# ple_gate's sixth product, right columns: its sums of weights made in DRAM during the output projection, not grown from the second product's

## The chip, the cores and the metric

The kernel runs on one core of one Trainium2 chip. The metric is the device time of one execution in microseconds; lower is better.

## The reference

One layer of a trunk: 512 tokens, width 2048, all in float32. Cut to the two matrix products that matter here, sliding-window attention ends in an output projection, and a gate with a second weight matrix of the same size follows.

```python
x = x + (out * silu(gate)) @ w_out            # [512,2048] @ [2048,2048]: the output projection
emb = p @ ple_proj                            # [512,256] @ [256,2048]
g = sigmoid(rmsnorm(x, ple_norm) @ ple_gate)  # [512,2048] @ [2048,2048]: the ple_gate product
x = x + emb * g
return rmsnorm(x, final_g)
```

## The kernel before

**Stages.** The kernel projects q, k, v and the gates and runs the attention between these products (to about 450 us), then does the output projection with `w_out` (450 to 621 us), then the product with `ple_gate` (621 to about 771 us), and stores the rows. In the second half PE works without a break through one list of pieces.

**Seven products instead of eight.** Each of the two big products is cut into 2x2 blocks and made by seven block products (Strassen's scheme in Winograd's form). Each block product needs a sum or difference of blocks of the activations and of the weights. The products are numbered 1 to 7; product 2 is left to a second level of the same scheme (`Small`, pieces half as long). The others run in the order `ORDER_OUT = ORDER_PLE = (1, 7, 6, 5, 3, 4)`; for each there is a left column half (`jj` = 0) and a right one (`jj` = 1), and for each half four pieces of weights (`m` = 0 to 3) of 128x1024 elements, 512 KB. So "7,1,2" is product 7, right columns, third piece. A full piece feeds 12 matmuls of 128x512, a small one 6.

**How a piece comes to PE.** The weights are float32 and the matmuls take a rounded high part and a remainder. A piece is loaded by a DMA on SP's queue (L752), rounded on ScalarE (`bhi`, L760, called ACT below), subtracted on VectorE (`blo`, L761, DVE below), and used by PE (L126 to L128). `Pieces.get(i)` and `Pieces.ahead(i)` write this order out by hand: the split is issued two pieces ahead of PE, loads three to six ahead. The high and the low part have three buffers each, so the split of piece n can begin when PE has finished piece n-3.

**Where a raw piece lies.** A piece of the kind "one" (`braw`) goes to `wraw` (three buffers) or, for every fourth, to a single buffer `fourth`: a ring of four, so that the load of a `braw` waits until the `blo` of the fourth `braw` before it has read its buffer. In a stretch of the output projection eight buffers called `grown` are used instead. Pieces of the kinds "seed" and "grow" lie in the `grown` buffers in the gate product: a "seed" is loaded once by SP, and a "grow" adds another block of weights onto that tile by an accumulating DMA on GpSimd's queue (L739, `accum_op=ALU.add`; POOL below), as soon as the `blo` of the earlier piece has read it.

**The sums of weights.** Winograd's sums of weight blocks for some products are made in DRAM during the attention: SP copies one block into a fresh DRAM tile, POOL adds a second by an accumulating DMA (`sum_weights`, lists `copies` and `adds`). For `ple_gate` this holds for products 7 and 5 (`SUMS`). The sum for 6 is the one for 7 plus one block, and the one for 4 is the one for 6 plus one more; before the change, both are grown in SBUF, for both column halves:

```python
growing = () if nm == "w_out" else (7, 6, 4)
kind = "one" if p not in growing else "seed" if p == growing[0] else "grow"
```

In the trace the eight seeds of product 7 are the rows `grown<-ple_gate` on SP, and the sixteen grows are the rows `grown<-in_ple_gate` on POOL: the first eight make product 6's sums (four left, four right), the last eight product 4's.

**Who sets the order.** PE's and SP's order is written by hand in all of this; POOL's order in the output projection up to product 4 is left to a scheduler, and is written by hand in the gate product after product 1. In the output projection a helper `todo()` runs once after each piece (`step` 0 to 3) and issues side work there: the loads of `x`, and the parts of a third, smaller product (`Embedding`, with accumulating DMAs on POOL and its results stored by POOL to the tiles `embeds`).

**Names in the rows below.** `braw`, `bhi`, `blo`: a piece raw, high, low. `g`, `smallg`, `o`: PSUM tiles of the gate product, of its second level, and of the output projection. `s`: side tiles. `hT`, `fhg`, `flg`: the activations' sums and their split. `e<-embeds`: the third product's results read back.

Of the kernel before, what the change touches and what calls it, by code (L numbers as in the profile page):

```python
# [11 lines left out]
F32 = mybir.dt.float32  # L12
F32R = mybir.dt.float32r
AF = mybir.ActivationFunctionType
ALU = mybir.AluOpType
# [5 lines left out]
P = 128  # L21
# [34 lines left out]
def trunk_kernel(ctx: ExitStack, tc: tile.TileContext, a: dict):  # L56
    nc = tc.nc
# [28 lines left out]
    WE = 1024  # L86
# [71 lines left out]
    def run(gen):  # L158
        for _ in gen:
            pass  # L160
# [38 lines left out]
    for k in range(KC):  # L199
# [67 lines left out]
        f, e = k == 0, k == KC - 1  # L267
# [416 lines left out]
    summed, copies, adds = {}, [], []  # L684

    def block(nm, r, c, jj, m):

        r = r if nm == "w_out" else 3 - r
        return a[nm][2 * (c - 1) + jj, 4 * (r - 1) + m]

    SUMS = [("w_out", 7), ("w_out", 5), ("w_out", 6), ("w_out", 4), ("ple_gate", 7), ("ple_gate", 5)]
    BASE = {7: (1, 2), 5: (1, 1), 6: 7, 4: 6}
    MORE = {7: (2, 2), 5: (1, 2), 6: (1, 1), 4: (2, 1)}

    def small_block(nm, r, c, m):

        return block(nm, 2, 1, c - 1, 2 * (r - 1) + m)

    def sum_small(nm, q):

        for m in range(2):
            t = summed["small", nm, q, m] = tc.dram_tile([P, WE], F32, name=f"small_{nm}_{q}_{m}")
            copies.append((t, small_block(nm, *BASE[q], m) if q in (7, 5) else summed["small", nm, BASE[q], m]))
            adds.append((t, small_block(nm, *MORE[q], m)))

    for nm, p in SUMS:
        for q in (6, 5) if (nm, p) == ("ple_gate", 5) else (p,):
            sum_small(nm, q)
        for jj in range(2):
            for m in range(4):  # L710
                t = summed[nm, p, jj, m] = tc.dram_tile([P, WE], F32, name=f"{nm}_{p}_{jj}_{m}")
                copies.append((t, block(nm, *BASE[p], jj, m) if p in (7, 5) else summed[nm, BASE[p], jj, m]))
                adds.append((t, block(nm, *MORE[p], jj, m)))
    sum_small("ple_gate", 4)
    SUM_STEPS = 2 * len(copies) + 6
    SUMS_EARLY = 16

# [85 lines left out]
    def add_stage(nm, order):  # L803
        at = {}

        for p in order:
            for jj in range(2):
                at[p, jj] = []
                for m in range(4):
                    at[p, jj].append(len(B.specs))  # L810
                    if (nm, p) in SUMS:
                        src = summed[nm, p, jj, m]
                    else:
                        src = block(nm, *{1: (1, 1), 3: (2, 2), 6: (1, 1), 4: (2, 1)}[p], jj, m)
                    growing = () if nm == "w_out" else (7, 6, 4)
                    kind = "one" if p not in growing else "seed" if p == growing[0] else "grow"
                    B.add(kind, src, (nm, jj, m) if p in growing else None)
                    if nm == "w_out" and (p, jj, m) in EMBED_AT:
                        at.setdefault("embed", []).append(len(B.specs))
                        B.add("emb", None)  # L820
                    for q in SMALL[nm].get((p, jj), {}).get(m, ()):
                        v = at.setdefault(("small", q), [])
                        src = summed.get(("small", nm, q, len(v)))
                        if src is None:
                            src = small_block(nm, *{1: (1, 1), 2: (2, 1), 3: (2, 2)}[q], len(v))
                        v.append(len(B.specs))
                        B.add("one", src)
        return at
# [6 lines left out]
        (6, 1, 0), (6, 1, 1), (6, 1, 3), (5, 0, 0), (5, 0, 2), (5, 0, 3), (5, 1, 1), (5, 1, 2), (3, 0, 0),  # L835
    ]
    at_out = add_stage("w_out", ORDER_OUT)
    at_ple = add_stage("ple_gate", ORDER_PLE)

    seeds = [n for n, (kind, _, _) in enumerate(B.specs) if kind == "seed"]  # L840
# [71 lines left out]
    def sums_in(i):  # L912
# [4 lines left out]
        if i < 4:  # L917
            return range(4 * i + 3, min(4 * i + 7, SUMS_EARLY), 2)
        n, of = SUM_STEPS - SUMS_EARLY, blocks - 4
        return range(SUMS_EARLY + (i - 4) * n // of, SUMS_EARLY + (i - 3) * n // of)  # L920
# [8 lines left out]
    for i in range(blocks + 3):  # L929
# [15 lines left out]
        for n in range(max(todo, 6)):  # L945
            if n < todo:
                next(proj)
            if n == 0:
                first_chores(i, 1)
                some(W.todo)  # L950
                some(chores or idle)
            elif n == 2:
                next(turned, None)
                next(value, None)
                if len(chores) > 1:
                    some(chores)
            elif n == 3:
                next(softmax, None)
            elif n == 4:
                first_chores(i, 2)  # L960
                some(chores or idle)
            elif n == 5:
                next(softmax, None)
# [37 lines left out]
    def unit(p, jj, at, forms, todo, between=lambda m, ps: None):  # L1001

        ps = banks(p, jj, forms.nm)
        f = forms.made[p]
        first = p not in (6, 5, 3)
        for m in range(4):
            bh, bl = B.get(at[p, jj][m])
            for kk in range(2):
                k = 2 * m + kk
                fh, fl = f[m]  # L1010
                for tb in range(2):
                    mm3(ps[tb], fh[:, kk, blk(tb)], fl[:, kk, blk(tb)], bh[kk], bl[kk], first and k == 0, k == 7, not first)
            some_later(4 - m)
            todo()
            between(m, ps)
        return ps


    def load_x(j, queue):
        queue.dma_start(x1[j], a["x"].rearrange("(t p) d -> p t d", p=P)[:, :, j * 512 : (j + 1) * 512])  # L1020
# [77 lines left out]
    def turns_due(at):  # L1098
        for part, j, th in turns_at.get(at, ()):
            part(j, th)  # L1100
# [262 lines left out]
            add_to_x(j, t, sign, ps)  # L1363

    turns = []


    load_x(0, nc.gpsimd)
# [5 lines left out]
    for n, p in enumerate(ORDER_OUT):  # L1374
        if p == 4:
            last_out.enter_context(
                tc.manual_schedule(
                    engines={getattr(mybir.EngineType, v) for v in ("PE", "SP", "Activation")}
                )
            )  # L1380
        nxt = out_forms.steps(ORDER_OUT[n + 1]) if n < 5 else iter(())
        for jj in range(2):
            later.extend(held.pop(waiting.get((p, jj)), ()))
            calls = iter(range(4))

            def between(m, ps):
                if (p, jj, m) in EMBED_AT:
                    embedding.slot()
                q = small_steps.get((p, jj, m))
                if q is not None:  # L1390
                    small_out.prepare(q)
                for q in SMALL["w_out"].get((p, jj), {}).get(m, ()):
                    small_out.product(q)

            def todo():
                step = next(calls)
                part = x_at.get((p, jj, step))
                if part is not None:
                    load_x(part, nc.sync)
                part = embed_steps.get((p, jj, step))  # L1400
                if part is not None:
                    embedding.prepare(part)
                next(nxt, None)
                if p == 4:
                    turns_due((p, jj, step))
                    if (jj, step) in ((0, 1), (0, 2), (0, 3), (1, 0)) and squares_due:
                        squares_due.pop(0)()
                if (p, jj) == (4, 1):
                    for _ in range(2 if step >= 2 else 0):
                        turn(*turns.pop(0), "o")  # L1410
                        next(ple_first, None)

            ps = unit(p, jj, at_out, out_forms, todo, between)
            posts = [partial_of(add_y, p, jj, tb, ps[tb]) for tb in range(2)]
            if p == 1:
                held[p, jj] = posts
            elif (p, jj) == (3, 1):
                later.insert(0, lambda both=posts: [post() for post in both])
            else:
                later.extend(posts)  # L1420
        run(nxt)
        if p == 3:
            turns = [(kp, 0) for kp in range(4)]
# [230 lines left out]
    f = ple_forms.made[4]  # L1654
# [166 lines left out]
```

## Time and profile before

| | |
|---|---|
| median of 3 runs | 781.82 us (781.66 to 782.34) |
| the profiled execution itself | 782.2 us |
| its span, first to last instruction | 780.5 us |
| PE busy | 770.5 us, 99% of the span |
| DVE, ACT, POOL busy | 79%, 68%, 21% |
| DMA on SP's queue (q1) | 154.58 MB, 56.3% of 16 engines |
| DMA on POOL's queue (q0) | 57.74 MB, 35.4% of 16 engines |
| accumulating loads into `grown` tiles | 16, 512 KB each, 10.2 us median to landing |
| seeds into `grown` tiles | 8, 512 KB each, 10.1 us median to landing |

How to read it: PE is nearly always busy, so time is lost or won only where PE stops or where the tail is. Within the 780.5 us the DMA share tells how far the 16 DMA engines are loaded; a share near 1 means that a transfer issued now waits for those ahead of it.

### The profile page before, as it was taken

The numbers are of one execution on the slowest core, as the hardware profiler recorded it, in microseconds if no ns is written. First come the engines' busy times: TensorE is split into PE (matmuls) and PEld (weight loads), VectorE is DVE, ScalarE is ACT, GpSimd is POOL, SyncE is SP. The second block draws the span as 40 slices with busy tenths as digits, with TensorE's granted clock in tenths as the row PEclk, the third lists the DMA queues.
The fourth block names the chain that finished last, engine by engine and source line by source line (L and its number), as shares of the span: only waits on it lengthen the run. The fifth ranks groups of instructions, "written<-read, shape, count | busy, mean of one in ns | idle before, by whom it ended". The sixth has DMA issues, their size and how long they took to land.

```text
span 780.5 us, 11140 instructions
## 1 busy us (share of the span) xinstructions
PE 770.5 (99%) x3652; PEld 644.0 (83%) x3652; DVE 618.4 (79%) x1069; ACT 529.0 (68%) x1121; POOL 167.4 (21%) x303
## 2 busy tenths in 40 slices
PE   9999999999999999999999999999999999999995
PEld 8888888888888888888888888888888888887884
DVE  4537697876978688777877799967799889988995
ACT  6734586766776676766766664577766888866974
POOL 0201523122232313132332100002111122221111
PEclk9999999999999999999999999999999999999998
DMA  9988899999999989999997589968799999999966
GB/s 347 289 215 302 183 264 310 287 290 271 276 260 275 273 241 276 278 282 265 261 286 213 139 302 317 303 213 284 245 392 331 318 283 294 274 278 309 330 147 216
DMA packets 52411, 213.02 MB, mean 273 GB/s; under 512 B 7985, under 2 KB 9009, under 8 KB 46593
## 3 DMA queue, kind: packets, MB, share of 16 engines
q1 hardware_dynamic: 39152, 154.58, 56.3%
q0 software_dynamic: 13200, 57.74, 35.4%
q8 instruction: 29, 0.48, 0.2%
q14 instruction: 30, 0.24, 0.1%
HBM read 195.45 MB, written 78.69 MB: 351 GB/s over the span
## 4 chain that ended last, share of the span: by engine, by line
PE 94%; DVE 2%; DMA 1%; issue 1%; ACT 0%; POOL 0%; POOLq 0%; DVEq 0%; ACTq 0%
PE gps L126 7%; PE gps L127 7%; PE gps L128 7%; PE qps L126 7%; PE qps L128 7%; PE qps L127 7%; PE o L126 6%; PE o L127 6%; PE o L128 6%; PE g L127 4%; PE g L128 4%; PE g L126 4%; PE s L485 2%; PE vps L290 2%; PE o L603 2%; PE pt L551 2%
## 5 line engine op out<-in xcount | busy, mean ns | idle before, releaser
L761 DVE TENSOR_TENSOR blo<-braw,bhi 128x1024 fp32r<-128x1024 f32 x100 | 121.5, 1220 | 22.5 <-ACT bhi L760 21.6
L760 ACT CAST bhi<-braw 128x1024 fp32r<-128x1024 f32 x100 | 105.1, 1052 | 47.9 <-PE o L128 18.3
L126 PE MATMUL gps<-xh,whi 128*128 128x512 f32 x256 | 100.0, 390 | 0.0
L127 PE MATMUL gps<-xl,whi 128*128 128x512 f32 x256 | 100.0, 390 | 0.0
L128 PE MATMUL gps<-xh,wlo 128*128 128x512 f32 x256 | 99.8, 390 | 0.0
L126 PE MATMUL qps<-xh,whi 128*128 128x512 f32 x224 | 87.8, 392 | 0.0
L128 PE MATMUL qps<-xh,wlo 128*128 128x512 f32 x224 | 87.5, 390 | 0.0
L127 PE MATMUL qps<-xl,whi 128*128 128x512 f32 x224 | 87.4, 390 | 0.0
L575 POOL TENSOR_SCALAR_AFFINE_SELECT own<-r 64x512 fp32r<-64x512 f32 (+1 forms) x48 | 32.5, 677 | 238.4 <-DVE r L565 221.8
L110 DVE TENSOR_TENSOR wlo<-wraw,whi 128x1024 fp32r<-128x1024 f32 x60 | 73.5, 1226 | 3.8 <-ACT whi L109 3.7
L126 PE MATMUL o<-bhi,fho 128*128 128x512 f32 x192 | 74.8, 390 | 0.0
L127 PE MATMUL o<-blo,fho 128*128 128x512 f32 x192 | 74.7, 389 | 0.0
L128 PE MATMUL o<-bhi,flo 128*128 128x512 f32 x192 | 74.7, 389 | 0.0
L109 ACT CAST whi<-wraw 128x1024 fp32r<-128x1024 f32 x60 | 62.3, 1039 | 5.7 <-issue 4.1
L127 PE MATMUL g<-blo,fhg 128*128 128x512 f32 x160 | 62.4, 390 | 0.3 <-DVE blo L761 0.3
L126 PE MATMUL g<-bhi,fhg 128*128 128x512 f32 x160 | 62.3, 390 | 0.0
L128 PE MATMUL g<-bhi,flg 128*128 128x512 f32 x160 | 62.3, 389 | 0.0
L128 PEld LDWEIGHTS gps<-xh,wlo 128*128 128x128 f32 x256 | 48.1, 188 | 10.3
L126 PEld LDWEIGHTS gps<-xh,whi 128*128 128x128 f32 x256 | 48.1, 188 | 9.2
L529 ACT ACTIVATE t<-t,sm 128x129 f32<-128x129 f32 (+1 forms) x128 | 49.6, 389 | 8.7 <-DVE sm L525 7.4
L127 PEld LDWEIGHTS gps<-xl,whi 128*128 128x128 f32 x256 | 48.1, 188 | 8.8
L564 ACT CAST r<-pt 128x256 fp32r<-128x256 f32 x56 | 20.9, 372 | 49.8 <-PE pt L551 49.3
(297 smaller groups left out, 1828.0 us busy)
## 6 DMA issues: line engine op xcount, KB each, us to landing
wraw<-in_w_gate_in SPq DMA_DIRECT2D x32, 512.0 KB, 8.3
w_out<-in_w_out POOLq DMA_DIRECT2D x32, 512.0 KB, 9.0
braw<-w_out SPq DMA_DIRECT2D x32, 512.0 KB, 6.0
wraw<-in_w_q SPq DMA_DIRECT2D x28, 512.0 KB, 6.6
braw<-in_w_out SPq DMA_DIRECT2D x22, 512.0 KB, 5.7
braw<-in_ple_gate SPq DMA_DIRECT2D x22, 512.0 KB, 7.3
xw<-in_first SPq DMA_DIRECT2D x14, 640.5 KB, 6.5
w_out<-in_w_out SPq DMA_DIRECT2D x16, 512.0 KB, 11.1
```

What stands on the lines that cost most here:

```text
L109: nc.scalar.copy(hi, raw)
L110: nc.vector.tensor_sub(lo, raw, hi.bitcast(F32))
L126: nc.tensor.matmul(ps, sh, mh, start=first, stop=False, skip_group_check=more)
L127: nc.tensor.matmul(ps, sh, ml, start=False, stop=False, skip_group_check=more)
L128: nc.tensor.matmul(ps, sl, mh, start=False, stop=last, skip_group_check=more)
L290: nc.tensor.matmul(v_ps[t], h[:, c], part_of(high_at, 256, 512), start=f, stop=e, skip_group_check=True)
L485: nc.tensor.matmul(s_ps[:, u, : 2 * n], st, of_keys[:, first * 2 * QB : (first * QB + n) * 2], start=True, stop=True)
L529: nc.scalar.activation(su, su, AF.Exp, bias=sm[:, u : u + 1], accum_out=sm[:, 2 + u : 3 + u])
L564: nc.scalar.copy(rh, src)
L575: nc.gpsimd.affine_select(out=flat(own), in_=flat(r).bitcast(F32), pattern=[[0, 8], [sign, HB]], compare_op=ALU.is_ge, fill=0.0, base=-HB ...
L760: nc.scalar.copy(hi[:, :n], raw)
L761: nc.vector.tensor_sub(lo[:, :n], raw, hi[:, :n].bitcast(F32))
```

## The change

For the right columns (`jj` = 1) the sum of product 6 is no longer grown from product 7's seed. It is made in DRAM, during the output projection, by four copies on SP and four accumulating DMAs on POOL. In the gate product the four right pieces of product 7 become plain pieces ("one"), the four right pieces of product 6 become the seeds, and only product 4 is grown on those. The left columns stay as they were. The number of DMAs on SP grows by eight; on POOL four are added and four taken away. No instruction of PE, ACT or DVE is added or removed; on ACT and DVE the four right pieces of product 7 are read from a `braw` buffer instead of a `grown` one.

```diff
+    for m in range(4):
+        summed["ple_gate", 6, 1, m] = tc.dram_tile([P, WE], F32, name=f"ple_gate_6_1_{m}")
...
-                    if (nm, p) in SUMS:
+                    if (nm, p, jj, m) in summed:
                         src = summed[nm, p, jj, m]
...
-                    growing = () if nm == "w_out" else (7, 6, 4)
+                    growing = () if nm == "w_out" else (6, 4) if (nm, 6, jj, m) in summed else (7, 6, 4)
...
+    sum_copies = [(6, 0, 1), (6, 1, 0), (6, 1, 3), (5, 0, 2)]
+    sum_adds = [(6, 0, 3), (6, 1, 2), (5, 0, 1), (5, 1, 0)]
...
+                if (p, jj, step) in sum_copies:
+                    m = sum_copies.index((p, jj, step))
+                    nc.sync.dma_start(summed["ple_gate", 6, 1, m], summed["ple_gate", 7, 1, m])
+                if (p, jj, step) in sum_adds:
+                    m = sum_adds.index((p, jj, step))
+                    nc.gpsimd.dma_start(
+                        summed["ple_gate", 6, 1, m], block("ple_gate", *MORE[6], 1, m), accum_op=ALU.add, max_dma_last_dim=8192
+                    )
```

The order on SP in the output projection, product 6, before (the number behind `braw` is the piece's place in the whole list of pieces; `s7` are loads for the third product):

```order
L752 DMA braw22_5433<-w_out_6_1_1_799 128x1024
L1238 DMA s7_5054<-in_ple_proj 128x512
L1239 DMA s7_5054<-in_ple_proj 128x512
L752 DMA braw24_5499<-w_out_6_1_2_800 128x1024
L752 DMA braw25_5519<-w_out_6_1_3_801 128x1024
L752 DMA braw27_5559<-w_out_5_0_0_784 128x1024
```

The same place now:

```order
L754 DMA braw22_5437<-w_out_6_1_1_799 128x1024
L1406 DMA ple_gate_6_1_0_836<-ple_gate_7_1_0_818 16x8192
L1240 DMA s7_5058<-in_ple_proj 128x512
L1241 DMA s7_5058<-in_ple_proj 128x512
L754 DMA braw24_5504<-w_out_6_1_2_800 128x1024
L754 DMA braw25_5525<-w_out_6_1_3_801 128x1024
L1406 DMA ple_gate_6_1_1_837<-ple_gate_7_1_1_819 16x8192
L754 DMA braw27_5566<-w_out_5_0_0_784 128x1024
```

Two of the four copies stand between the loads here, the other two likewise a few pieces on; each pushes the loads behind it.

The order on SP in the gate product, around product 7's right pieces (pieces 88, 90, 92, 93), before:

```order
L752 DMA braw86_6870<-small_ple_gate_7_1_813 128x1024
L752 DMA grown88_6872<-ple_gate_7_1_0_818 128x1024
L752 DMA braw87_6899<-small_ple_gate_6_0_822 128x1024
L752 DMA grown90_6912<-ple_gate_7_1_1_819 128x1024
L752 DMA braw89_6937<-small_ple_gate_6_1_823 128x1024
L752 DMA grown92_6958<-ple_gate_7_1_2_820 128x1024
L752 DMA braw91_6971<-in_ple_gate 128x1024
L752 DMA grown93_6973<-ple_gate_7_1_3_821 128x1024
L752 DMA braw94_7025<-in_ple_gate 128x1024
L752 DMA braw96_7064<-small_ple_gate_5_0_824 128x1024
L752 DMA braw99_7116<-small_ple_gate_5_1_825 128x1024
```

The same place now, from piece 87 on:

```order
L754 DMA braw87_6909<-small_ple_gate_6_0_822 128x1024
L754 DMA braw88_6922<-ple_gate_7_1_0_818 128x1024
L754 DMA braw89_6947<-small_ple_gate_6_1_823 128x1024
L754 DMA braw90_6968<-ple_gate_7_1_1_819 128x1024
L754 DMA braw91_6981<-in_ple_gate 128x1024
L754 DMA braw92_6996<-ple_gate_7_1_2_820 128x1024
L754 DMA braw93_7025<-ple_gate_7_1_3_821 128x1024
L754 DMA braw94_7037<-in_ple_gate 128x1024
L754 DMA braw96_7075<-small_ple_gate_5_0_824 128x1024
L754 DMA braw99_7125<-small_ple_gate_5_1_825 128x1024
L754 DMA grown102_7146<-ple_gate_6_1_0_836 128x1024
L754 DMA braw101_7158<-small_ple_gate_4_0_834 128x1024
```

Pieces 88, 90, 92 and 93 have moved into the ring of four `braw` buffers, so the load of each piece here waits for an earlier one: 90 for the `blo` of 86, 91 for that of 87, 92 for that of 88, 93 for that of 89. The new seeds (102, 104, 106, 107) follow between the small pieces of products 5 and 4.

The order on POOL in the gate product, the accumulating DMAs from product 6's right pieces on, before (`grown88` to `grown93` are the tiles of the right columns):

```order
L739 DMA grown85_6564<-in_ple_gate 128x1024
L739 DMA grown88_6872<-in_ple_gate 128x1024
L739 DMA grown90_6912<-in_ple_gate 128x1024
L739 DMA grown92_6958<-in_ple_gate 128x1024
L739 DMA grown93_6973<-in_ple_gate 128x1024
L739 DMA grown81_6471<-in_ple_gate 128x1024
```

The same place now:

```order
L741 DMA grown85_6576<-in_ple_gate 128x1024
L741 DMA grown81_6483<-in_ple_gate 128x1024
```

Four accumulating DMAs have gone from between product 6's left pieces and product 4's.

The order on POOL in the output projection, now (before, the rows of L1409 are not there and the rest stands in this order):

```order
L1409 DMA ple_gate_6_1_0_836<-in_ple_gate 64x2048
L1244 DMA s7_5058<-in_ple_proj 128x512
L1245 DMA s7_5058<-s1_5056 128x512
L1409 DMA ple_gate_6_1_1_837<-in_ple_gate 64x2048
L1309 DMA embeds1_0_5059<-made1_1_5606 128x1024
L1409 DMA ple_gate_6_1_2_838<-in_ple_gate 64x2048
L1309 DMA embeds5_0_5061<-made5_3_5707 128x1024
L1309 DMA embeds3_0_5063<-made3_2_5671 128x1024
L1257 DMA s7_5058<-in_ple_proj 128x512
L1409 DMA ple_gate_6_1_3_839<-in_ple_gate 64x2048
L1258 DMA s7_5058<-s1_5056 128x512
L1309 DMA embeds4_0_5065<-made4_4_5780 128x1024
```

Each of the four adds waits on POOL for its copy on SP, with the third product's DMAs queued behind it.

## The prediction

> **What bounds the kernel now.** I read the page first, then the windows of the second half, PE's waits, PE's timeline at the one wait found, and the chain behind it. The page says (busy time of PE; then the chain of work that ended last, by engine):
>
> ```profile
> PE 770.5 (99%) x3652; PEld 644.0 (83%) x3652; DVE 618.4 (79%) x1069; ACT 529.0 (68%) x1121; POOL 167.4 (21%) x303
> PE 94%; DVE 2%; DMA 1%; issue 1%; ACT 0%; POOL 0%; POOLq 0%; DVEq 0%; ACTq 0%
> ```
>
> PE is busy for all but 10 us of the span of 780.5 us. Where these 10 us lie, the windows tell (stretch, its length, busy time of PE, PEld, DVE, ACT, POOL, granted clock, DMA share, GB/s), and PE's waits:
>
> ```profile
> 680.00:720.00 40.00, 39.70 (x176) 32.52 (x175) 34.84 (x42) 25.84 (x35) 10.14 (x11) 1.00 1.05 295
> 760.00:780.50 20.50, 11.62 (x74) 10.46 (x72) 12.53 (x27) 9.63 (x20) 2.10 (x3) 0.88 0.58 206
> PE warm_ps L141 <- PEq L1811: 0.8, 1, 0.8
> PE g L127 <- DVE blo L761: 0.3, 1, 0.3
> ```
>
> 8.9 us are the tail after 760 us, where rows are scaled and stored, 0.8 us the start. Between them PE has one idle moment, in the gate product. Ends of matmuls are modelled, so I measure it by starts, on PE's timeline (start, length, instruction): the first two rows are the first matmuls of two pieces without a stop, the third and the last those of pieces 112 (product 5, left, fourth piece) and 113.
>
> ```profile
> 668.36 0.39 PE L126 MATMUL g<-bhi,fhg 128*128 128x512 f32 x1
> 671.08 0.39 PE L126 MATMUL g<-bhi,fhg 128*128 128x512 f32 x1
> ...
> 713.24 0.39 PE L126 MATMUL g<-bhi,fhg 128*128 128x512 f32 x1
> 713.93 0.50 PE L127 MATMUL g<-blo,fhg 128*128 128x512 f32 x1 [0.30 <-DVE blo L761]
> ...
> 716.60 0.39 PE L126 MATMUL g<-bhi,fhg 128*128 128x512 f32 x1
> ```
>
> A piece lasts 671.08 - 668.36 = 2.72 us; piece 112 lasted 716.60 - 713.24 = 3.36 us. So 0.64 us is lost there, and it is all that better supply of weights can win in this trace: 0.64 / 781.8 = 0.08%. About 0.2% (1.56 us) is what a measurement of this kernel can tell from no change. The cause is in the chain, with ACT's row for piece 112's high part:
>
> ```profile
> 696.12 11.28 DMA braw<-ple_gate
> 707.50 1.06 ACT bhi L760
> 711.30 1.05 ACT L760 CAST bhi<-braw 128x1024 fp32r<-128x1024 f32 x1 [2.75 <-DMA braw<-ple_gate]
> ```
>
> The loads of 512 KB take 11 us and ACT waits for them. That is a queue, not the transfer. These windows show it, with POOL's first and last grows before and after the right columns' four (645.74 is the first of sixteen, 653.84 the fourth, 673.89 the ninth, 699.86 the last):
>
> ```profile
> 646.00:650.00 4.00, 4.00 (x19) 3.30 (x18) 3.98 (x5) 3.74 (x7) 1.54 (x2) 1.00 1.03 400
> 650.00:652.00 2.00, 2.00 (x10) 1.69 (x9) 1.35 (x2) 2.00 (x5) 0.85 (x1) 1.00 1.09 225
> 674.00:711.00 37.00, 37.00 (x165) 30.62 (x164) 32.27 (x39) 22.77 (x29) 10.00 (x11) 1.00 1.05 276
> ...
> 645.74 0.93 POOL L739 DMA_DIRECT2D grown<-in_ple_gate  x1 [6.67 <-issue]
> 653.84 0.85 POOL L739 DMA_DIRECT2D grown<-in_ple_gate  x1 [1.98 <-DVE blo L761]
> 673.89 0.85 POOL L739 DMA_DIRECT2D grown<-in_ple_gate  x1 [2.35 <-DVE blo L761]
> 699.86 0.87 POOL L739 DMA_DIRECT2D grown<-in_ple_gate  x1 [1.47 <-DVE blo L761]
> ```
>
> With loads alone (646 to 650 us) the engines move 400 GB/s, so a piece of 0.524 MB takes 1.31 us. With the first grow nearly alone (650 to 652 us) they move 225 GB/s: 2.33 us for one. With both queues filled (674 to 711 us) 276 GB/s: a load and a grow together take 3.80 us, and in that state SP gets one load through per 3.80 us. The share is above 1 throughout.
>
> The Trainium skill ("DMA: Bandwidth & Descriptors", section "Anatomy of one DMA — SWDGE (gpsimd) path") fits a DMA from GpSimd as 2.0 us plus its bytes at 436 GB/s, with no term for accumulating. By that an estimate for a grow would be 1.2 us of movement, as for a plain load, and trading grows for loads would free nothing; the row of 225 GB/s disagrees.
>
> **The change, part by part.** *Eight DMAs in the output projection.* The trace has no row of such a copy beside this stage's work; I bound one between a load (1.31 us) and a grow (2.33 us), and an add between 2.33 and 3.80 us: together 4 x 3.64 to 4 x 6.13, 15 to 25 us of DMA time. What lies free there, and what covers the loads behind the copies (SP's load of piece 29, ACT's row that reads it, longest load of the stretch 488 to 545 us):
>
> ```profile
> 480.00:520.00 40.00, 40.00 (x178) 33.12 (x177) 34.26 (x45) 24.20 (x33) 2.30 (x3) 1.00 0.84 280
> 520.00:560.00 40.00, 40.00 (x178) 33.15 (x177) 30.50 (x39) 30.36 (x49) 6.71 (x11) 1.00 0.75 250
> 504.65 0.42 SPq L752 DMA_DIRECT2D braw<-w_out  x1
> 523.10 1.05 ACT L760 CAST bhi<-braw 128x1024 fp32r<-128x1024 f32 x1
> DMA to landing us min/median/max: 3.3/5.7/8.5
> ```
>
> Free are 0.16 x 40 + 0.25 x 40 = 16.4 us, so the stage gets full but the work fits nearly. The load of piece 29 lands by 513.2 us at the latest and is read at 523.10: 10 us of cover, from the eight `grown` buffers; two copies ahead of a load push it by at most 4.7 us. On POOL each add waits for its copy, and behind it stand the third product's accumulating DMAs and stores; an add holds them for 3.80 us at most, and the loads that need a stored buffer have the same cover. I take 0. If the cover were gone, each copy would show with its 1.3 to 2.3 us.
>
> *Four right pieces of product 7 in the ring of four.* Their loads can no longer start early: each waits for an earlier `blo`. The gates are in rows of before: SP's issue of 654.71 us waited for piece 86 and that of 657.30 for piece 87 (the first of four in that row); the `blo` of 88 and 89 are DVE's rows. ACT's rows are the high parts of pieces 90, 91, 92 and 93, the last line the landings of `braw` from 600 to 725 us:
>
> ```profile
> 654.71 0.33 SPq L752 DMA_DIRECT2D braw<-in_ple_gate  x1
> 657.30 14.58 SPq L752 DMA_DIRECT2D braw<-small_ple_gate  x4
> 658.93 1.22 DVE L761 TENSOR_TENSOR blo<-grown,bhi 128x1024 fp32r<-128x1024 f32 x1
> 660.13 1.22 DVE L761 TENSOR_TENSOR blo<-braw,bhi 128x1024 fp32r<-128x1024 f32 x1
> 660.40 1.06 ACT L760 CAST bhi<-grown 128x1024 fp32r<-128x1024 f32 x1 [0.30 <-PE smallg L128]
> 663.42 1.04 ACT L760 CAST bhi<-braw 128x1024 fp32r<-128x1024 f32 x1
> 664.48 1.06 ACT L760 CAST bhi<-grown 128x1024 fp32r<-128x1024 f32 x1
> 668.10 1.04 ACT L760 CAST bhi<-grown 128x1024 fp32r<-128x1024 f32 x1
> DMA to landing us min/median/max: 3.2/8.7/14.9
> ```
>
> A load by itself takes 3.2 us, 1.9 of them not transfer. Piece 90, issued at 654.71, shares with a grow: 654.71 + 1.9 + 3.80 = 660.4, when ACT read it before. Are grows still under way after that? The left columns' four start to move at 650; four at 2.33 and two loads at 1.31 end at 662. After 662 POOL's queue is empty until the ninth grow of 673.89, since the four grows of the right columns are gone. So 91 lands at about 663, 92 (issued at 658.93 + 1.22 = 660.15) at 664.3, 93 (issued at 661.35) at 665.6, against ACT's 663.42, 664.48 and 668.10. Latest harmless starts on ACT are PE's start minus 2.3 us (1.06 + 1.22): 666.0 for 92 and 668.7 for 93. I take 0. The upper bound has a grow beside each load: 92 at 660.4 + 2 x 3.80 = 668.0, 2.0 us late, 93 at 671.8, 3.1 us late. ACT and DVE would wait in order, with the activations' splits queued behind, and PE would wait 3.1 us in all.
>
> *Four grows gone, four seeds new, in the gate product.* From 662 to 677 us (the ninth grow is issued at 673.89; the first moved its bytes near 650, some 3 to 4 us after its issue) SP has the queue alone. Ten loads fall into it: pieces 92, 93, 94, 96, 99, 101, 103 and the seeds 102, 104, 106; 10 x 1.31 = 13.1 us, of 15. From 677 on come eight grows, and up to piece 112 nine loads (`e` twice; 105, 107, 108, 109 to 112): 8 x 3.80 + 1.31 = 31.7, so 112 lands at 708.7. Before it landed at 711.2 (ACT's 711.30). Harmless is 713.24 - 2.3 = 710.9. So the stall goes, -0.64 us, with 2.2 us to spare. What is late next is nothing of DMA: the next pieces have the same gain. One load more that falls behind the ninth grow costs 3.80 - 1.31 = 2.5 us: then 112 lands at 711.2 again and the 0.64 us stay. That is the lower and the upper bound of this term, -0.64 and 0, with up to 2.5 us for a second such load.
>
> The sum for the profiled execution: 782.2 (span 780.5 and 1.7 around it) + 0 + 0 - 0.64 = 781.6 us. The median lies 0.4 us lower, 781.82, so 781.2 us.
>
> **The rivals.** *The stall stays.* The DMA engines are full before and after; in sum the gate product trades four grows for four loads, 4 x (2.33 - 1.31) = 4 us less work, and some of that can be lost in moments when the ring has no load to issue. For it: the margin of 2.2 us is smaller than the price of one misplaced load. Against it: at 276 GB/s and a share of 1.05 from 674 to 711 us SP's loads were paired with grows nearly all the time, and now begin that stretch without a backlog. Time: 781.8 us. By the skill's fit it would be this case too, in which a grow costs no more than a load.
>
> *The ring holds product 7's right pieces back (slower).* The place is pieces 91 to 93, near 665 us; the price 0 to 3.1 us as worked out. It decides when the left columns' grows are still moving at 664 us rather than 662, since then 92 comes past 666.0. For it: the 8.7 us median to landing in the row above, and that these pieces could be loaded early and now can't. Against it: 8.7 us is 1.9 plus nearly twice 3.80, so two loads queued, and the ring has one to two here. With 3.1 us, and the old stall gone since all else is early by then, 781.2 + 3.1 = 784.3 us; a middle case 782.7 us.
>
> *The change does nothing or wins elsewhere.* The tail could shift by its own; nothing in the rows says so, since its 8.9 us come after the last grow.
>
> **How the numbers follow.** Forecast (stall gone, no new one) 0.54: 781.2 us. Stall stays 0.26: 781.8. Ring 0.17: 781.5 to 784.3, 0.11 of it above 783.4. Something else that wins over 0.2% 0.03. So faster by over 0.2%: 0.03; within: 0.54 + 0.26 + 0.06 = 0.86; slower: 0.11. The range runs from 780.8 (the forecast less 0.4 us, about half of what the three runs span) to 783.0, which takes in the second case and the cheaper half of the ring's.
>
> **What would show it.** Right: on PE no start later than 0.32 us after the one before in the gate product; ACT's wait for `braw<-ple_gate` (5.8 us before, near 710) gone or moved; twelve grows on POOL with a hole from 662 to 674 us. Wrong: a wait of PE or ACT for `braw` near 664 to 669 us (the ring), ACT waiting at 707 to 711 us as before (no gain), or waits for `braw<-w_out` between 490 and 545 us (the cover is gone).

## The result and the profile after

The changed kernel takes 788.32 us, median of 6 runs (787.77 to 789.39), against 782.08 us of the kernel before, run beside it (6 runs, 781.66 to 783.37). The ratio is 1.0079, 95% interval 1.0066 to 1.0092: the change makes the kernel slower by 6.2 us. The forecast was 781.2 us with a range up to 783.0, so the result lies 5.3 us above the end of the range. Of all runs below, one of the kernel "seeds behind piece 94" took 858.38 us at a granted clock of 0.849; it counts in no ratio, and without it the median there is 783.87 us.

The profiled execution took 789.39 us with a span of 787.7 us, 7.2 us more than before. The page of the changed kernel (busy time of the engines; the chain of work that ended last):

```profile
PE 773.9 (98%) x3652; PEld 645.1 (82%) x3652; DVE 618.4 (79%) x1069; ACT 528.9 (67%) x1121; POOL 167.2 (21%) x303
PE 89%; DMA 4%; DVE 3%; issue 2%; ACT 2%; POOL 0%; POOLq 0%; DVEq 0%; ACTq 0%
```

No engine has more instructions to do, but the chain now has 4% DMA where it had 1%: PE waits for weights. Where, the waits of PE tell (us in total, times, longest), and its timeline (start, length, instruction; in brackets the idle time ahead of it and its releaser):

```profile
PE g L127 <- DVE blo L763: 2.7, 4, 0.8
PE g L126 <- ACT bhi L762: 0.9, 1, 0.9
PE smallg L127 <- DVE blo L763: 0.5, 1, 0.5
```

```profile
645.45 0.44 PE L126 MATMUL g<-bhi,fhg 128*128 128x512 f32 x1
646.65 0.50 PE L127 MATMUL g<-blo,fhg 128*128 128x512 f32 x1 [0.76 <-DVE blo L763]
...
665.61 0.49 PE L126 MATMUL g<-bhi,fhg 128*128 128x512 f32 x1
666.86 0.50 PE L127 MATMUL g<-blo,fhg 128*128 128x512 f32 x1 [0.76 <-DVE blo L763]
...
669.53 0.39 PE L126 MATMUL smallg<-bhi,small_ahg 128*128 128x512 f32 x1
670.40 0.50 PE L127 MATMUL smallg<-blo,small_ahg 128*128 128x512 f32 x1 [0.48 <-DVE blo L763]
...
708.25 0.39 PE L128 MATMUL smallg<-bhi,small_alg 128*128 128x512 f32 x1
709.57 0.50 PE L126 MATMUL g<-bhi,fhg 128*128 128x512 f32 x1 [0.93 <-ACT bhi L762]
710.83 0.50 PE L127 MATMUL g<-blo,fhg 128*128 128x512 f32 x1 [0.76 <-DVE blo L763]
...
712.13 0.63 PE L128 MATMUL g<-bhi,flg 128*128 128x512 f32 x1
712.55 0.63 PE L126 MATMUL g<-bhi,fhg 128*128 128x512 f32 x1
...
715.03 0.39 PE L126 MATMUL g<-bhi,fhg 128*128 128x512 f32 x1
...
720.50 0.39 PE L126 MATMUL g<-bhi,fhg 128*128 128x512 f32 x1
721.27 0.50 PE L127 MATMUL g<-blo,fhg 128*128 128x512 f32 x1 [0.38 <-DVE blo L763]
```

Starts should follow each other by 0.227 us (2.72 us for 12). The rows are the first matmuls of pieces 81, 90, 91, 109 and 112. Lost are 0.97 us at 645, 1.02 at 665, 0.64 at 669, and 0.54 at 720. Between 708.25 and 715.03 lie 13 starts, 6.78 us instead of 2.95: 3.83 us lost, in two stops and then in matmuls that follow each other by 0.42 us. Of these 3.83 us, 4.20 - 11 x 0.227 = 1.7 us fall after 710.83, in the slow matmuls. Together 7.0 us, less the 0.64 us of before: 6.4 of the 7.2 us by which the span grew. The rest is in delays too small to place (the second matmul after a stop is late by 0.1 us too).

The stretches that carried the prediction, first of before, then of after (PE, PEld, DVE, ACT, POOL busy, granted clock, DMA share, GB/s):

```profile
662.00:677.00 15.00, 15.00 (x68) 12.41 (x67) 13.64 (x17) 13.72 (x23) 3.41 (x4) 1.00 1.06 275
668.00:677.00 9.00, 9.00 (x42) 7.44 (x41) 7.64 (x9) 8.06 (x14) 2.24 (x3) 1.00 1.06 271
```

```profile
662.00:677.00 15.00, 13.76 (x59) 10.54 (x58) 11.87 (x14) 11.71 (x20) 0.00 (x0) 1.00 0.77 268
668.00:677.00 9.00, 8.52 (x38) 6.62 (x37) 8.78 (x11) 8.21 (x15) 0.00 (x0) 1.00 0.70 237
```

Between 662 and 677 us the prediction had SP fill the DMA engines with ten loads at 400 GB/s. The engines were idle for a quarter of that time (share 0.77): 268 GB/s x 15 us = 4.0 MB, less than eight pieces of 0.524 MB, and part of that was the last grow.

What SP did in that stretch is in its own rows (start, length, load; a row x2 or x4 stands for several, the length then runs to the last). They are piece 94; 96 and 99; the first seed, 102; the fourth, 107; and pieces 109 to 112:

```profile
666.84 0.33 SPq L754 DMA_DIRECT2D braw<-in_ple_gate  x1
670.37 1.46 SPq L754 DMA_DIRECT2D braw<-small_ple_gate  x2
671.88 0.42 SPq L754 DMA_DIRECT2D grown<-ple_gate  x1
...
680.48 0.56 SPq L754 DMA_DIRECT2D grown<-ple_gate  x1
...
690.62 13.92 SPq L754 DMA_DIRECT2D braw<-ple_gate  x4
```

From 666.84 to 670.37 SP issues nothing: 96 needs the ring's buffer that the `blo` of 91 reads, and that is late. The seeds need no buffer of the ring, their `grown` tiles have long been free, but they stand behind 96 in the queue. The first is issued at 671.88, the fourth at 680.48.

Why the `blo` of 91 is late, the tiles' landing times show (from issue; min, median, max), of the ring's loads 89 to 91, of the left columns' four grows, and, for what comes later, of the load of piece 109; behind them the chain's step for piece 90:

```profile
DMA to landing us min/median/max: 7.0/7.2/8.4
DMA to landing us min/median/max: 5.6/8.1/9.3
DMA to landing us min/median/max: 17.8/17.8/17.8
```

```profile
656.02 8.38 DMA braw<-ple_gate
```

ACT's rows for 109 and 110:

```profile
708.47 1.04 ACT L762 CAST bhi<-braw 128x1024 fp32r<-128x1024 f32 x1 [5.54 <-DMA braw<-ple_gate]
712.33 1.04 ACT L762 CAST bhi<-braw 128x1024 fp32r<-128x1024 f32 x1 [1.57 <-DMA braw<-ple_gate]
```

Piece 90 landed at 656.02 + 8.38 = 664.4, not at 660.4, and PE's stop of 665.61 is its own; 91 came behind it. Of these 4.0 us 1.3 are a later issue (656.02 for 654.71, behind PE's stop at 645 us) and 2.7 a longer load (8.4 us for 1.9 + 3.80). Piece 109 was issued at 690.62 and landed at 708.4; piece 110 came 3.86 us later, so in that state one load gets through per 3.86 us.

### The profile page after: what moved, and what is told of

Read it like the earlier page. It is cut to its first block, busy times and chain, and to the rows that moved or that the text cites. A ratio compares the mean times of both kernels' runs of the same rounds, so it can differ in the third digit from the quotient of the medians.

```text
span 787.7 us, 11152 instructions
## 1 busy us (share of the span) xinstructions
PE 773.9 (98%) x3652; PEld 645.1 (82%) x3652; DVE 618.4 (79%) x1069; ACT 528.9 (67%) x1121; POOL 167.2 (21%) x303
## 4 chain that ended last, share of the span: by engine, by line
PE 89%; DMA 4%; DVE 3%; issue 2%; ACT 2%; POOL 0%; POOLq 0%; DVEq 0%; ACTq 0%
PE gps L126 7%; PE gps L127 7%; PE gps L128 7%; PE qps L126 7%; PE qps L128 7%; PE qps L127 7%; PE o L126 6%; PE o L127 6%; PE o L128 6%; DMA braw<-ple_gate 3%; PE g L127 2%; PE g L128 2%; PE g L126 2%; PE s L485 2%; PE vps L290 2%
## 5 line engine op out<-in xcount | busy, mean ns | idle before, releaser
L763 DVE TENSOR_TENSOR blo<-braw,bhi 128x1024 fp32r<-128x1024 f32 x104 | 126.1, 1219 | 29.5 <-ACT bhi L762 28.7
L762 ACT CAST bhi<-braw 128x1024 fp32r<-128x1024 f32 x104 | 109.0, 1051 | 53.0 <-PE o L128 18.0
```

Source lines behind the costliest of these rows:

```text
L762: nc.scalar.copy(hi[:, :n], raw)
L763: nc.vector.tensor_sub(lo[:, :n], raw, hi[:, :n].bitcast(F32))
```

## The experiments

**The theories.** The main theory, formed from these rows, has two faults that follow from each other. First, loads 89 to 91 move beside the left columns' grows, land late, and PE stops at 665 and 669 us. Second, since each ring load waits for an earlier `blo`, this lateness goes into SP's queue, the seeds behind it come late, fall beside product 4's eight grows, and push 109 to 112 back: PE stops at 708 to 721 us. Rivals: the eight DMAs in the output projection cost the time; or the order on SP alone delays the seeds, whatever the grows do; or the ring of four alone is too short.

| kernel | median us (runs) | before beside it | ratio, 95% interval |
|---|---|---|---|
| after | 788.32 (6) | 782.08 | 1.0079, 1.0066 to 1.0092 |
| DRAM sums made, not used | 782.50 (11) | 782.38 | 1.0004, 0.9995 to 1.0013 |
| sums loaded over the old tile | 781.88 (11) | 782.38 | 0.9997, 0.9989 to 1.0006 |
| seeds behind piece 94 | 783.88 (11) | 782.38 | 1.0018, 1.0009 to 1.0028 |
| seeds behind piece 86 | 785.18 (8) | 782.38 | 1.0043, 1.0028 to 1.0058 |
| no left grows | 786.54 (4) | 782.51 | 1.0053, 1.0038 to 1.0068 |
| seeds behind 94, no left grows | 782.28 (10) | 782.51 | 0.9992, 0.9981 to 1.0002 |
| no grows of product 4 | 783.46 (10) | 782.51 | 1.0017, 1.0008 to 1.0026 |

**The sums in DRAM, read by nobody.** The eight DMAs stay in the output projection; the gate product is as before.

```diff
-                    if (nm, p, jj, m) in summed:
+                    if (nm, p) in SUMS:
...
-                    growing = () if nm == "w_out" else (6, 4) if (nm, 6, jj, m) in summed else (7, 6, 4)
+                    growing = () if nm == "w_out" else (7, 6, 4)
```

> The gate product as before (product 6's right sums grown on product 7's seeds), but with the four copies and four accumulating DMAs of the change in the output projection; their tiles are read by nobody. Main theory (the loss sits in the gate product: ring of four, seeds behind it on SP's queue): as before, 782.1 us within 0.5, at most 1.1 more if the wait of PE at 645 us that the changed kernel shows comes with it. Rival one (the eight DMAs crowd the output projection and the delay is carried on): 785 us or more.

Measured: 782.50 us, no difference from before. The windows of the output projection are those that the prediction showed of before, stretch by stretch:

```profile
480.00:520.00 40.00, 40.00 (x179) 33.10 (x178) 33.75 (x45) 23.82 (x33) 3.96 (x5) 1.00 1.01 335
520.00:560.00 40.00, 40.00 (x178) 33.14 (x177) 30.50 (x40) 30.36 (x49) 8.37 (x13) 1.00 0.90 291
```

In the gate product PE has one wait, the old one (in total, times, longest):

```profile
PE g L127 <- DVE blo L763: 0.2, 1, 0.2
```

The DMA share rises from 0.84 to 1.01 and from 0.75 to 0.90, which is 0.17 x 40 + 0.15 x 40 = 13 us of DMA time, and PE stays busy for all 80 us. So the copies and adds are paid for and hidden. The whole loss comes from the gate product.

**The new sums, loaded onto the old tiles.** Product 7's right pieces stay seeds in `grown` buffers, as before; product 6's right sums are loaded by SP from DRAM onto the same tiles once these are read, at the place in the program where the grow was issued before. No piece moves into the ring.

```diff
+            elif kind == "over":
+                t = self.grown[key]
+                nc.sync.dma_start(t, src)
...
-                    growing = () if nm == "w_out" else (6, 4) if (nm, 6, jj, m) in summed else (7, 6, 4)
+                    growing = () if nm == "w_out" else (7, 6, 4)
                     kind = "one" if p not in growing else "seed" if p == growing[0] else "grow"
+                    if (nm, p, jj) == ("ple_gate", 6, 1):
+                        kind = "over"
```

> The changed kernel, but product 7's right pieces stay seeds in grown buffers, loaded early, and product 6's right sums are loaded by SP onto the same tiles once read, in place of the accumulating DMAs. No piece enters the ring of four. Main theory: both groups of waits go, 781.5 to 782.6 us. Rival one: 785 us or more. Rival two: 781.5 to 783 us.

Measured: 781.88 us, not to be told from before. The only wait of PE behind the one at its start, and the window of 668 to 677 us:

```profile
PE qps L277 <- ACT xh L230: 0.2, 1, 0.2
```

```profile
668.00:677.00 9.00, 9.00 (x41) 7.44 (x41) 7.64 (x10) 8.05 (x14) 0.87 (x1) 1.00 0.90 305
```

The wait is in the first projections, not in the gate product: even the stop of before is gone. So sums from DRAM do what the prediction said of them, when the ring is left alone; and there was no more to win than the 0.64 us, too little for the runs to show.

**The four new seeds earlier.** The changed kernel, with its four new seeds issued together behind piece 94, ahead of the loads that wait for the ring; and a second one with them behind piece 86 (82 in place of 90).

```diff
+            if i >= 90:
+                for n in seeds[4:]:
+                    if n not in self.base and n >= self.done:
+                        self._prepare(n)
```

> The changed kernel, but SP issues the four new seeds together right behind piece 94, ahead of piece 96. Main theory: they go through in the hole of the DMA engines near 668 to 677 us, the loads of pieces 109 to 112 land some 8 us earlier, PE's waits at 708 to 715 us and the half clock go (4.5 us), those at 665 to 670 us stay: about 783.8 us (783 to 785). Rival two (the ring's waits alone push everything late, the place of the seeds does not matter): 787 to 788 us. Rival one: 787 to 788 us.

> The changed kernel, but SP issues the four new seeds together right behind piece 86, where the old seeds of product 7 began. Main theory: the waits at 708 to 715 us go as well, those at 665 to 670 us stay or grow a little, since pieces 87 and 88 land 5 us later: 783.5 to 785 us. Rival two: 787 to 788 us.

Measured behind 94: 783.88 us. PE's waits, SP's row for the four seeds, and the window:

```profile
PE g L127 <- DVE blo L763: 0.8, 1, 0.8
PE smallg L127 <- DVE blo L763: 0.5, 1, 0.5
```

```profile
666.70 2.15 SPq L754 DMA_DIRECT2D grown<-ple_gate  x4
```

```profile
668.00:677.00 9.00, 8.48 (x37) 6.64 (x37) 8.46 (x11) 8.27 (x15) 0.33 (x1) 1.00 1.02 401
```

The hole in the DMA share is filled (1.02 for 0.70), the waits at 708 to 721 us and the slow matmuls are gone, and two waits stay, those at 665 and 669 us. So of the 6.2 us, 6.2 - 1.5 = 4.7 us hang on when the seeds are issued, and 1.5 us on something ahead of it.

Measured behind 86: 785.18 us, a little over what was expected. The eight runs fall apart: five took 784.17 to 785.40 us, three 787.39 to 788.45, and the profiled one is the slowest of all. So its rows show what can happen there, not what the median pays. In it the seeds landed between 646 and 651 us and pushed the ring's loads 87 to 90 back instead, which then meet the left grows. PE's rows there, and the clock:

```profile
665.82 0.39 PE L128 MATMUL smallg<-bhi,small_alg 128*128 128x512 f32 x1
667.34 0.52 PE L126 MATMUL g<-bhi,fhg 128*128 128x512 f32 x1 [1.13 <-ACT bhi L762]
668.60 0.80 PE L127 MATMUL g<-blo,fhg 128*128 128x512 f32 x1 [0.74 <-DVE blo L763]
```

```profile
669.00:675.00 6.00, 6.00 (x16) 4.66 (x16) 6.00 (x10) 5.51 (x8) 0.00 (x0) 0.54 0.62 200
```

A load moved forward is thus not free. The changed kernel has a gap in the DMA engines there too (shares of 0.58 and 0.74 from 645 to 648 and 651 us), but it is about 2 us long, and four loads take 4 x 1.31 = 5.2 us: what does not fit takes the place of another load.

**Without the left columns' four grows.** The grows of product 6's left sums are not issued.

```diff
-                nc.gpsimd.dma_start(t, src, accum_op=ALU.add)
+                if i not in at_ple[6, 0]:
+                    nc.gpsimd.dma_start(t, src, accum_op=ALU.add)
```

> The changed kernel without the four accumulating DMAs that make product 6's left sums (the products 6 left and 4 left are then computed with unfinished sums; PE, ACT, DVE and SP issue what they issued). Main theory: these four grows land at 652.7, 656.9, 660.6 and 664.5 us in the changed kernel, and they are why the ring's loads 89, 90 and 91 take 7 to 8 us; from there the lateness goes on through SP's queue to the new seeds and to the loads at 680 to 712 us, which then stand beside the last eight grows. Without them a load takes 3.2 to 5 us, the seeds land by 677 us, and both groups of waits (665 to 670 and 708 to 721 us) go: 781.4 to 782.4 us. Rival, the order on SP alone (seeds behind loads that wait for a ring buffer): only the first waits of 1.9 us go, the seeds stay behind and the waits at 708 to 721 us stay: 786 to 787.5 us.

Measured: 786.54 us, so here the main theory failed and the order on SP alone was right. The loads from 650 to 663 us (min, median, max), PE's waits, SP's rows for pieces 94, 96 with 99, and the first seed, and the window:

```profile
DMA to landing us min/median/max: 3.2/3.5/4.7
```

```profile
PE g L127 <- DVE blo L764: 2.3, 3, 1.0
```

```profile
664.31 0.33 SPq L755 DMA_DIRECT2D braw<-in_ple_gate  x1
667.84 1.46 SPq L755 DMA_DIRECT2D braw<-small_ple_gate  x2
669.35 0.42 SPq L755 DMA_DIRECT2D grown<-ple_gate  x1
```

```profile
668.00:677.00 9.00, 9.00 (x42) 7.44 (x41) 7.64 (x10) 8.03 (x15) 0.94 (x1) 1.00 0.87 299
```

The first half of the theory holds: without these grows a ring load takes 3.5 us (median of these five) instead of 7.2 (of 89 to 91), and the stops at 665 and 669 us are gone (one of the three waits left is at 646 us, two are at 712 and 716 us). The second half does not: the seeds still stand behind 96, which is issued at 667.84 although no load is late: the `blo` of 91 runs two pieces ahead of PE and gives its buffer back only then. The share stays at 0.87, and the late waits stay, smaller in the profiled execution (785.14 us, the lowest of the four; what the other three lost beyond it has no trace). The left grows' lateness adds to the second fault; it is not its cause.

**The same, with the seeds behind piece 94.** Both edits together.

> The changed kernel with the four new seeds right behind piece 94 (783.9 us with its waits at 665 to 670 us), and without the four accumulating DMAs of product 6's left sums (the products 6 left and 4 left are then computed with unfinished sums). Main theory: the remaining 1.9 us at 665 to 670 us are the grows that move beside the loads 90 and 91: they go, 781.4 to 782.2 us. Rival, the ring of four by itself is too short for the four right pieces of product 7: the waits stay, 783.5 to 784.2 us.

Measured: 782.28 us, the main theory's range but for 0.1 us, and clear of the rival's 783.5. The window, and the only wait of PE behind the one at its start:

```profile
668.00:677.00 9.00, 9.00 (x42) 7.44 (x41) 7.64 (x10) 8.04 (x13) 0.94 (x1) 1.00 1.02 412
```

```profile
PE qps L277 <- ACT xh L230: 0.2, 1, 0.2
```

So the ring of four is long enough for product 7's right pieces where its loads move alone. The two faults roughly add up: with the seeds moved alone 1.5 us are left, without the left grows alone 4.0 us, together 5.5 of the 6.2 us, and with both edits nothing that the runs can tell.

**Without the eight grows of product 4.** As above, with `at_ple[4, 0] + at_ple[4, 1]` in the condition, on the changed kernel itself.

> The changed kernel without the last eight accumulating DMAs, those of product 4's sums (product 4 is then computed with unfinished sums). Main theory: the waits at 665 to 670 us come before these grows and stay (1.9 us); the seeds are late as before, but the loads behind them cost 1.31 us each and not 3.85 us, so 109 lands by 697 us and the waits at 708 to 721 us go, the half clock with them: 783.4 to 784.4 us. Rival, the seeds' lateness on SP alone makes the later loads late: 786.5 to 788.5 us.

Measured: 783.46 us. PE's waits, and the landing times of pieces 109 to 112:

```profile
PE smallg L127 <- DVE blo L764: 0.5, 1, 0.5
PE g L127 <- DVE blo L764: 0.4, 1, 0.4
```

```profile
DMA to landing us min/median/max: 3.2/3.3/3.4
```

Both waits are the ones near 665 and 669 us. The seeds are as late as in the changed kernel, but a load takes 3.3 us where 109 took 17.8, and nothing stops at 708 us. Late seeds cost time only because what stands behind them moves beside grows.

## Why the prediction was wrong, point by point

*The bound and what can be won.* Right. PE is the bound, and only 0.64 us were to be had: with the sums loaded over the old tiles the stop is gone and the median does not move measurably.

*The eight DMAs in the output projection: 0.* Right. The estimate was 15 to 25 us of DMA time; the share shows 13 us more between 480 and 560 us, where the engines are then nearly full. The cover held.

*The ring: "I take 0", bound 3.1 us.* Wrong in size, inside its bound. The step that failed is "654.71 + 1.9 + 3.80 = 660.4", one grow beside one load. Loads 89 to 91 took 7.0 to 8.4 us. Beside that of 90 two grows were under way at once, and from 658.62 on the load of 91 too; the last of the four grows was issued at 655.16 and landed at 664.5. Without these grows the load of 90 took 3.5 us. The rival named the point from which this decides, left grows still moving at 664 us rather than 662, and that came true; it was given 0.17. What it cost is about 1.5 us. The row that spoke for it, 8.7 us median to landing, was read as two queued loads and explained away.

*"Ten loads fall into it … 112 lands at 708.7 … the stall goes."* This is the step that lost the prediction. It filled a hole in the DMA engines by counting bytes, 13.1 us of loads into 15 us of time, and never asked when SP could issue them. Seven of the ten were ring loads, each waiting for the `blo` of the fourth `braw` before it, and the new seeds, which wait for nothing, stood behind them in the same queue. By 677 us five of the ten had landed (92, 93, 94, 96, 99). The share of 0.70 where 1.0 was assumed is this mistake in one number; putting the seeds ahead of the waiting loads brings it to 1.02 and gives 4.7 of the 6.2 us back. The listing of SP's order ahead of the prediction has the seeds behind the ring loads; what was missing was to read it with the gates.

*"One load more that falls behind the ninth grow costs 3.80 - 1.31 = 2.5 us."* This does not follow from the prediction's own sum. "8 x 3.80 + 1.31" has eight pairs for nine loads, so a tenth load moves alone and puts 112 back by 1.31 us; but a load that comes in ahead of a piece that is still paired puts that piece back by a whole pair, 3.86 us by ACT's two rows. No run tests either size by itself. In the changed kernel 109 landed at 708.4 us, against 699.8 before, and 112 at 716.0, against the 708.7 of the forecast. The 8.6 us of 109 are a little over two pairs and not five, since four of the five late loads had landed by 682.2 us, before the ninth grow, issued at 677.23 (673.89 before), landed at 686.4.

*The half clock* was not in the prediction at all. It is 1.7 of the 7.2 us in the profiled execution. The other five runs have no trace, but their mean granted clock is on record. It is 0.995 in the profiled run, 0.993 in one, 0.996 in three and 0.997 in one; the runs of the kernel before show 0.996 to 0.998, and 3.5 us at half clock take 0.5 x 3.5 / 787 = 0.002 off the mean. So the run at 0.997 can hardly have had it, and it took 788.61 us all the same. For the three at 0.996 it stays open.

*The wait at 645 us* is not explained. It stands in the trace of the changed kernel (0.97 us) and of that without left grows, but not in the one with unused DRAM sums, nor in that without product 4's grows, which has the same instructions up to there as the first two. The loads of pieces 79 and 80 landed at 638.7 and 640.0 us in the changed kernel, at 637.7 and 640.2 without left grows, and at 636.5 and 637.8 without product 4's grows, and piece 81, split behind them, has no slack there. A wait that comes and goes between executions of the same instructions is not counted to the change here; why those loads differ stays open.

## What to carry to other kernels

A gap in the DMA engines is filled only by loads that may be issued in it: for each load write down which buffer it waits for and when that comes free, and for each load that waits for nothing, what waiting load stands ahead of it in its queue. Moving tiles from buffers with a long lead into a short ring therefore changes the times of all loads behind them, not only their own. Price a load that slips into a stretch of paired transfers at the pair (here 3.86 us) for every piece that is still paired behind it, and at its own time (here 1.31 us) past the last accumulating load. This price is argued from the times between landings; no run here tests it alone.

## What the runs showed of the hardware that was not expected

TensorE's clock halves after stops that are short. In the changed kernel PE was idle for 0.93 and 0.76 us within 2.6 us (708.25 to 710.83). From about 711.5 to 715 us matmuls followed each other by 0.42 to 0.43 us instead of 0.227. The profile shows a granted clock of 0.50 there:

```profile
712.00:713.00 1.00, 1.00 (x4) 0.71 (x4) 0.00 (x0) 0.67 (x1) 1.00 (x2) 0.50 1.07 270
```

With the seeds behind 86 the same came in the third of three stops of 1.2 to 1.5 us between starts, from 663.6 to 668.6 us: the granted clock was 1.00 from 667.0 to 667.5, 0.50 from 668.0 on, and the slow matmuls lasted until 674.6. Single stops of this size, at 645 and 665 us in the changed kernel, did not bring it. The Trainium skill ("TensorE: Matmul & The Clock Gate", Part 1: The HAM clock gate) says that the clock falls to half after an idle window of about 3.4 us and comes back after about 3.4 us of work. The 3.5 us at half clock in the changed kernel and the step between matmuls (426.7 ns there for 512 columns) agree with these rows; with the seeds behind 86 PE worked for 6.0 us, from 668.6 to 674.6, before the clock came back. That page also calls the window free-running, which no run here shows. The idle window does not agree: PE never stood still for 3.4 us here, and two stops of about 1 us, with one matmul between them, were enough, and the measurement decides.

A ring load beside the left columns' accumulating loads took 7.0 to 8.4 us to land, and 3.5 us (median) without them. The Trainium skill ("DMA: Bandwidth & Descriptors", section "Queues, rings and completion order") says that each engine takes turns between the queues that have work, a packet at a time. The 3.86 us between loads in a stretch with both queues filled is about what one load and one grow take together (3.80 us by the rate of 276 GB/s), which agrees with it.
